# One projection of a hybrid encoder layer by seven products instead of eight, its operands' sums made by accumulating DMAs

## The chip, the core and the metric

The kernel runs on one core of a Trainium2 chip. The metric is the device time of one execution in microseconds (us), taken as the median of several runs. A profile of one further execution shows what each engine did: TensorE (PE, with its weight loads as PEld), VectorE (DVE), ScalarE (ACT), GpSimd (POOL) and SyncE (SP), which issues most DMAs.

## What is computed

One layer on x of 1024 positions by 1024 channels, in float32. Cut to what the change touches, the reference is:

```python
proj = jnp.einsum("bsd,de->bse", h, w_in)          # h = rmsnorm(x)
a = ...                                            # convolution branch, to 1024 channels
o = _bi_hgrn2(q, v, z_f, z_b, lb[0], lb[1])        # 8 heads of 128, both directions
of = o * lax.rsqrt(jnp.mean(o * o, axis=-1, keepdims=True) + EPS)
bmix = of * norm_w * jax.nn.silu(og)
bmix = jnp.einsum("bse,ed->bsd", bmix, o_w)        # the o projection
y = jax.nn.sigmoid(g_a) * a + jax.nn.sigmoid(g_b) * bmix
x = x + jnp.einsum("bsd,de->bse", y, w_out)
...                                                # feed-forward block, final norm
```

## The kernel before

All activations are kept transposed: a tile has 128 channels on the partitions and 512 positions (one half of the sequence) along it. A product with a weight column of 128 channels is a sum over 8 tiles of channels. Float32 accuracy is had by splitting each operand into a high and a low part (`split`, L124: a cast on ScalarE, a subtraction on VectorE), and by three matmuls for each pair (`mm3`, L144: lines 149 to 151). The input projection and the feed-forward block already use seven products for a block of two by two (`pair_job`, L283), with sums of weights and of activations as operands; the o projection doesn't.

The program runs in stages. After the input projections come the scans: 8 heads, two halves each. Their matmuls are woven with pieces of the remaining input projections and of the convolution's last product (`dense`), and a head's outputs (`outputs`, `scan_outputs`) follow one head later. There, GpSimd places four blocks of a half's scores by four small DMAs (L1371, tile `S`), makes the norm factors (L575 and L576, tile `ors`), ScalarE scales by them (L1452), PE turns the tiles (L1460), and VectorE applies gain and gate (L1462). The result is written to `d_bm[h][half]` by SP, the last head's is split at once; `bm_loads` brings the other heads back and splits them.

The o projection follows (L1590 and on): a job for each of the 8 output tiles, for each half 8 rows of three matmuls into a bank `mm` of PSUM. `merge` (L1571) loads the gate `d_gb` and the gated convolution branch `d_a`, multiplies and adds on VectorE and splits the result into `mg`, which the w_out stage reads. Beside these jobs `weight_sums` makes the sums of weights for the first three jobs of the feed-forward block, by VectorE, and stores them in `d_us`.

The order on PE is the order of the program (L91). On the other engines a scheduler sets it when the kernel is built, and each engine then works through its list in order, its DMA issues included. `later(n, do)` (L159) puts work n pieces of the matmul stream ahead in the program; `run_jobs` (L195) prepares the next job's weights while one runs. Pools with a fixed number of buffers (`wr` and `wp` for weights, `hx`, `ev`, `tm` and others for tiles) let a new tile wait for the last reader of an old one.

Of the kernel before, what the change touches and what calls it, by code (L numbers as in the profile page):

```python
# [21 lines left out]
CONV_FILL = 1.53  # L22
NPAIRS = 19
LN_MEAN = 5
GLU_FIRST = 4
GLU_LEAD = 6
GLU_FILL = 2
# [21 lines left out]
def tile_hybrid_encoder(  # L49
# [74 lines left out]
    def split(hi, lo, src, eng, late=False):  # L124
        parts = A.copy(hi, src), eng.tensor_tensor(lo, src, hi.bitcast(F32), op=ALU.subtract)  # L125
# [438 lines left out]

    def in_cols(c0):
        return w_cols(w_in, 0, ND, c0)


    NK2 = ND // 2
# [625 lines left out]

    last_keys, last_turned, last_scaled = [], [], []

    kscale = cp.tile([P, 2 * NH], F32, name="kscale")
    V.tensor_scalar(kscale, lbw[:, 3, :], DK**-0.5, None, op0=ALU.mult)

# [214 lines left out]
    def scan_outputs(h, kept, Sf, Sb):  # L1415


        ons, gates = [None, None], [None, None]
        ss = cp.tile([P, 2, 4], F32, name=nm("oss"), tag="oss", bufs=2)
        rs = cp.tile([P, 2, 4], F32, name=nm("ors"), tag="ors", bufs=2)  # L1420
        for half in (1, 0):
            S_t, v, qF = kept[half]
            o = bank("ob")
            for c in range(4):
                sl = slice(c * P, (c + 1) * P)
                g = half * 4 + c
                terms = [(S_t[:, c, :], v[:, c, :])]
                if g > 0:
                    terms.append((qF[:, 1, sl], Sf[half][:, c, :]))
                if g < 7:  # L1430
                    terms.append((qF[:, 0, sl], Sb[half][:, c, :]))
                for n, (l, r) in enumerate(terms):
                    T.matmul(o[:, sl], l, r, start=(n == 0), stop=(n == len(terms) - 1))  # L1433
            on = tmp()
            A.copy(on, o)
            for c in range(4):
                junk = hp.tile([P, DK], F32, tag="jk", name=nm("jk"), bufs=1)
                A.activation(  # L1438
                    junk, on[:, c * P : (c + 1) * P], AF.Square, accum_out=ss[:, half, c : c + 1]
                )  # L1440
            ons[half] = on
            gates[half] = page(hp, "og", 2)
            nc.sync.dma_start(gates[half], d_og[h][half])
            if half == 1:
                yield
        rstd_small(rs, ss, DK)
        yield
        yield
        for half in range(2):
            for c in range(4):  # L1450
                sl = slice(c * P, (c + 1) * P)
                done = A.activation(  # L1452
                    ons[half][:, sl], ons[half][:, sl], AF.Copy, scale=rs[:, half, c : c + 1]
                )
            last_scaled[:] = [done]
            yield
        for half in range(2):
            b = bank("tr")
            for c in range(4):
                T.transpose(b[:, c * P : (c + 1) * P], ons[half][:, c * P : (c + 1) * P], ident)  # L1460
            bt = ev()
            V.scalar_tensor_tensor(bt, b, vec("hn", h), gates[half], op0=ALU.mult, op1=ALU.mult)  # L1462
            if h == NH - 1:
                bm[h][half] = split(hx(), hx(), bt, V)
            else:
                nc.sync.dma_start(d_bm[h][half], bt)
            yield

    class Base:
# [29 lines left out]
        yield  # L1499
        yield from scan_outputs(h, kept, Sf, Sb)  # L1500

    bm = [[None, None] for _ in range(NH)]

    def bm_loads(half):
        for h in range(NH - 1):
            t = page(hp, "A", 8)
            nc.sync.dma_start(t, d_bm[h][half])
            behind = last_turned if h < NH - 2 else last_scaled
            with tc.issue_after(behind[0].ins):
                bm[h][half] = split(hx(), hx(), t, V)  # L1510

    NI = 2 * NH
    cur = Base(scan_inputs(0))
# [42 lines left out]
    for steps, pieces in TAIL:  # L1556
        pending.fill(steps)
        dense.fill(pieces)
    bm_loads(0)
    pending.fill(1)  # L1560
    dense.drain()
    bm_loads(1)
    pending.drain()
    hp.release()

# [5 lines left out]
    def merge(i):  # L1571
        def evac(half, acc):
            sb, a = ev(), tmp()
            for t, src in ((sb, d_gb), (a, d_a)):
                nc.sync.dma_start(t, src[i][half])
            V.tensor_tensor(sb, acc, sb, op=ALU.mult)
            V.tensor_tensor(a, a, sb, op=ALU.add)
            mg[i][half] = split(
                page(p4, "mg", 4 * ND, F32R), page(p4, "mg", 4 * ND, F32R), a, V
            )  # L1580

        return evac

    def o_cols(i):
        return w_cols(hgrn_o_w, 0, NH, i * P)

    def bm_of(k, half):
        return bm[k][half]

    o_jobs = [duo_job(o_cols(0), o_cols(1), NH, bm_of, merge(0), merge(1))]  # L1590
    o_jobs += [std_job(o_cols(i), NH, bm_of, merge(i)) for i in range(2, ND)]

    def column_halves(w, r0, nk, c0, c1):
        return [w_cols(w, r0, 2 * nk, c) for c in (c0, c1)]

    def up_cols(j):
        return column_halves(ffn_w_up, 0, ND // 2, j * P, DFF + j * P)
# [4 lines left out]
    def weight_sums(r, o, nk, d):  # L1602
        cols = nk * P

        def piece(src=None):
            t = page(fw, "h7", 2 * NK2)[:, :cols]
            if src is not None:
                nc.sync.dma_start(t.rearrange("p (k e) -> p k e", e=P), src)
            return t

        r0, o0, o1, r1 = piece(r[:, :nk]), piece(o[:, :nk]), piece(o[:, nk:]), piece(r[:, nk:])

        def sums():
            c0 = piece()
            todo = ((c0, r0, o0), (o1, o0, o1), (r0, r0, o1), (r1, r1, r0))
            for q, (t, a, b) in enumerate(todo):
                V.tensor_tensor(t, a, b, op=ALU.add)
                nc.sync.dma_start(d[:, q], t)

        return sums  # L1620

    s_o = Stream(run_jobs(o_jobs))
    todo = [(*up_cols(n), ND // 2, d) for n, d in enumerate(d_us)]
    for n, args in enumerate(todo):
        s_o.fill(16 if n else 8)
        later(5, weight_sums(*args))
    s_o.drain()
    advance_chores(1 << 10)

# [497 lines left out]
```

## Time and profile before

| | |
|---|---|
| median of 3 runs | 1707.12 us (1706.96 to 1707.62) |
| the profiled execution | 1706.98 us |
| its span | 1705.0 us |
| PE busy | 1688.6 us, 11719 instructions |
| DVE, ACT, POOL busy | 1269.3, 827.3, 245.9 us |
| mean granted PE clock | 0.999 |
| moved by DMA | 306.17 MB, 180 GB/s |

A row of a timeline has the start in us, the duration, the engine, the line, the operation, the tiles written and read with a count, and in brackets the engine's idle time before it with what ended it. A line of the DMA table has what is written from what, the issuing engine, the number of issues, the size of one, and the median us from issue to landing. Line numbers are those of the kernel before unless the text says otherwise.

### The profile page before, as it was taken

To read this page: it belongs to the slowest core of one execution; us is meant where nothing else is said; L and a number is where in the kernel's file an instruction comes from. 1 tells how busy PE (TensorE), PEld (TensorE's weight loads), DVE (VectorE), ACT (ScalarE), POOL (GpSimd) and SP (SyncE) were. 2 spreads that over 40 slices of the span, in tenths; PEclk is the share of its full clock that TensorE was granted. 3 is DMA by queue.
4 is the path that set the end of the run, shared out by engine and by line. 5 is a ranking of instruction groups with operands and counts; after the bars stand their busy time and mean duration, and the time that the engine had idled before them with its cause. 6 is when DMAs were issued, how large, how long until landed. Compare 5 with 4: busy or idle time off the path is not lost.

```text
span 1705.0 us, 30406 instructions
## 1 busy us (share of the span) xinstructions
PE 1688.6 (99%) x11719; PEld 1408.2 (83%) x11719; DVE 1269.3 (74%) x1938; ACT 827.3 (49%) x1562; POOL 245.9 (14%) x287
## 2 busy tenths in 40 slices
PE   9999999999999999999999999999999999999998
PEld 6788888888888888888888888888888888888787
DVE  5889899887678888888565467676777776657865
ACT  7454343335476777776432345444344434442334
POOL 1312222200001111111100003122222222000110
PEclk9999999999999999999999999999999999999999
DMA  7887887866573444436797455686777776773842
GB/s 240 284 213 186 191 196 172 205 187 206 165 236 100 139 129 134 129 116 221 241 294 243 128 167 176 153 171 143 172 164 178 164 183 149 237 260 102 212 98 99
DMA packets 332871, 306.17 MB, mean 180 GB/s; under 512 B 17454, under 2 KB 244918, under 8 KB 332726
## 3 DMA queue, kind: packets, MB, share of 16 engines
q1 hardware_dynamic: 285366, 265.42, 48.8%
q0 software_dynamic: 47360, 38.81, 15.4%
q8 instruction: 92, 1.51, 0.4%
q14 instruction: 53, 0.43, 0.1%
HBM read 201.40 MB, written 84.93 MB: 168 GB/s over the span
## 4 chain that ended last, share of the span: by engine, by line
PE 70%; ACT 1%; DVE 1%; DMA 0%; issue 0%; POOL 0%; POOLq 0%; ACTq 0%; DVEq 0%
PE mm L149 16%; PE mm L151 16%; PE mm L150 16%; PE sc L149 3%; PE sc L150 3%; PE sc L151 3%; PE ob L1433 2%; PE tr L149 2%; PE tr L150 2%; PE tr L151 2%; PE sc L1247 1%; PE sc L1333 1%; PE mm L1392 1%; PE sc L1392 1%; PE ob L1247 1%; PE tr L1382 0%
## 5 line engine op out<-in xcount | busy, mean ns | idle before, releaser
L149 PE MATMUL mm<-hx,wp 128*128 128x512 f32 x1068 | 425.7, 399 | 0.0
L151 PE MATMUL mm<-hx,wp 128*128 128x512 f32 x1068 | 417.0, 390 | 0.5 <-DVE wp L125 0.5
L150 PE MATMUL mm<-hx,wp 128*128 128x512 f32 x1068 | 416.2, 390 | 0.6 <-POOL hx L125 0.6
L125 ACT CAST wp<-wr 128x1024 fp32r<-128x1024 f32 (+2 forms) x146 | 146.9, 1006 | 224.3 <-PE mm L150 165.0
L151 PEld LDWEIGHTS mm<-hx,wp 128*128 128x128 f32 x1068 | 200.5, 188 | 44.6 <-DVE wp L125 1.6
L149 PEld LDWEIGHTS mm<-hx,wp 128*128 128x128 f32 x1068 | 200.6, 188 | 40.6 <-ACT wp L125 0.2
L150 PEld LDWEIGHTS mm<-hx,wp 128*128 128x128 f32 x1068 | 200.8, 188 | 39.9 <-POOL hx L125 1.0
L125 DVE TENSOR_TENSOR wp<-wr,wp 128x1024 fp32r<-128x1024 f32 (+2 forms) x144 | 169.5, 1177 | 39.8 <-ACT wp L125 39.4
L1065 DVE SCALAR_TENSOR_TENSOR acc<-gl,v_b,acc 128x1024 f32<-128x1024 f32 x120 | 153.5, 1280 | 1.7
L441 ACT COPY su<-mm 128x512 f32<-128x512 f32 x82 | 47.8, 583 | 84.4 <-PE mm L151 84.3
L1371 POOL DMA_DIRECT2D S<-D x64 | 36.1, 571 | 281.1 <-ACT jk L1438 125.3
L125 ACT CAST wq<-sw 128x1024 fp32r<-128x1024 f32 x41 | 43.2, 1054 | 61.3 <-PE mm L150 32.9
L1194 DVE TENSOR_TENSOR qF<-qF,tb 128x512 f32<-128x512 f32 x96 | 65.9, 686 | 9.5 <-ACT A L1228 8.9
L149 PE MATMUL tr<-hx,wp 128*128 128x512 f32 x180 | 70.1, 390 | 0.0
L151 PE MATMUL tr<-hx,wp 128*128 128x512 f32 x180 | 70.1, 389 | 0.0
L150 PE MATMUL tr<-hx,wp 128*128 128x512 f32 x180 | 70.0, 389 | 0.0
L1194 DVE TENSOR_TENSOR kG<-kG,tb 128x512 f32<-128x512 f32 x96 | 65.9, 687 | 4.0 <-ACT A L1228 2.2
L1710 DVE SCALAR_TENSOR_TENSOR tm<-gp,v_a,tm 128x512 f32<-128x512 f32 x88 | 66.0, 750 | 3.3 <-ACT tm L1708 1.3
L302 POOL DMA_DIRECT2D sw<-in_ffn_w_up_dram x38 | 49.8, 1502 | 116.0 <-DMA sw<-in_ffn_w_up_dram 72.4
L149 PE MATMUL sc<-hy,wq 128*128 128x512 f32 x164 | 63.9, 390 | 0.0
L151 PE MATMUL mm<-hy,wp 128*128 128x512 f32 x164 | 63.8, 389 | 0.0
L149 PE MATMUL mm<-hy,wp 128*128 128x512 f32 x164 | 63.8, 389 | 0.0
(377 smaller groups left out, 3721.9 us busy)
## 6 DMA issues: line engine op xcount, KB each, us to landing
wr<-in_w_in_dram SPq DMA_DIRECT2D x48, 512.0 KB, 5.6
wr<-in_ffn_w_up_dram SPq DMA_DIRECT2D x22, 512.0 KB, 5.6
sw<-in_w_in_dram SPq DMA_DIRECT2D x38, 256.0 KB, 3.1
d_g<-ft SPq DMA_DIRECT2D x38, 256.0 KB, 2.0
sw<-in_ffn_w_up_dram SPq DMA_DIRECT2D x38, 256.0 KB, 3.2
sw<-in_ffn_w_up_dram POOLq DMA_DIRECT2D x38, 256.0 KB, 6.7
wr<-sw POOLq DMA_DIRECT2D x32, 256.0 KB, 3.2
wr<-wr POOLq DMA_DIRECT2D x32, 256.0 KB, 3.3
```

What stands on the lines that cost most here:

```text
L125: parts = A.copy(hi, src), eng.tensor_tensor(lo, src, hi.bitcast(F32), op=ALU.subtract)
L149: T.matmul(acc, whi[:, k, :], ahi, start=first, stop=False, skip_group_check=again)
L150: T.matmul(acc, whi[:, k, :], alo, start=False, stop=False, skip_group_check=again)
L151: T.matmul(acc, wlo[:, k, :], ahi, start=False, stop=last, skip_group_check=again)
L302: G.dma_start(o, a, accum_op=ALU.add)
L441: A.copy(t, acc)
L1065: V.scalar_tensor_tensor(acc, g[:, k : k + S], tap(k), acc, op0=ALU.mult, op1=ALU.add)
L1194: return V.tensor_tensor(o, a, b, op=op)
L1247: T.matmul(b[g, o], A_t[:, at : at + 32], Q_t(at), start=True, stop=True)
L1371: G.dma_start(S_t[g : g + 32, :, g : g + 32], D_t[g : g + 32])
L1392: T.matmul(u[:, sl], kTs[d][:, sl], v[:, c, :], start=True, stop=True)
L1710: V.scalar_tensor_tensor(c, g[:, o + k : o + k + H], vec("fdw", k * NF + j), c, op0=ALU.mult, op1=ALU.add,)
```

## The change

The o projection is written as seven products. With the operand's tiles in blocks (heads 0 to 3 and 4 to 7 by the two halves) and the weights in blocks (input rows by output columns), each product takes 4 rows for one of four pairs of output tiles (tile p and tile p + 4). They are run product by product over the four pairs: 1, 2 and 6 for all pairs, then 7 and 4 pair by pair, then 5 and 3. A group of two items shares one weight page.

- In the scan stage, `sums_by_dma` makes the sums of weights, for the four pairs (`d_os`) and the three feed-forward jobs (`d_us`), seven sums in all: a piece is loaded, other pieces are added to it by accumulating DMAs that GpSimd issues, and each sum is stored by SP. `weight_sums` is gone.
- The gains get signs (`less`), all heads' results go to `d_bm`, and `bm_loads` brings back one half only.
- The sums of activations are made in `chain` from `d_bm` by accumulating DMAs too (`plus`), each followed by a split (`operand`): product 7, then 6, then 4 from the same page, and 5 from another; 3 is a block as it is.
- Product 7 is copied by ScalarE, and product 4 accumulates in its bank. `merge` adds `d_a` by an accumulating DMA.

```diff
+    d_os = [dp.tile([P, 4, ND // 2 * P], F32, name=f"d_os_{n}") for n in range(ND // 2)]
...
-            V.scalar_tensor_tensor(bt, b, vec("hn", h), gates[half], op0=ALU.mult, op1=ALU.mult)
-            if h == NH - 1:
-                bm[h][half] = split(hx(), hx(), bt, V)
-            else:
-                nc.sync.dma_start(d_bm[h][half], bt)
+            gain = vec("hn", h) if (h < NK2) == (half == 1) else less[:, h : h + 1]
+            V.scalar_tensor_tensor(bt, b, gain, gates[half], op0=ALU.mult, op1=ALU.mult)
+            nc.sync.dma_start(d_bm[h][half], bt)
...
+    def sums_by_dma(at, r, o, d):
...
+        def piece(src):
+            t = hp.tile([P, NK2, P], F32, tag="ws", name=nm("ws"), bufs=2)
+            nc.sync.dma_start(t, src)
+            return t
...
+        def more(t, src):
+            G.dma_start(t, src, accum_op=ALU.add)
+        def keep(n, t):
+            nc.sync.dma_start(q(n), t)
+        todo = (
+            lambda: ts.extend((piece(a11), piece(a21))),
+            lambda: (more(ts[0], a21), more(ts[1], a22)),
+            lambda: (keep(0, ts[0]), keep(1, ts[1])),
+            lambda: more(ts[1], a11),
+            lambda: keep(2, ts[1]),
+            lambda: more(ts[1], a12),
+            lambda: keep(3, ts[1]),
+        )
+        for n, do in enumerate(todo):
+            later(at + SUMS_GAP * n, do)
...
+    def merge(e, p, half, x0, x1=None, op=None):
+        i = p + e * NK2
+        t = next(gates_of)()
+        nc.sync.dma_start(t, d_gb[i][half])
...
+            V.tensor_tensor(both, x0, x1, op=op)
+            V.tensor_tensor(t, both, t, op=ALU.mult)
+        G.dma_start(t, d_a[i][half], accum_op=ALU.add)
+        mg[i][half] = split(mg_page(), mg_page(), t, V)
...
+    def plus(t, src):
+        G.dma_start(t, src, accum_op=ALU.add)
...
+    for k in range(NK2):
+        chain.append(raw_page(d_bm[k][1]))
+        plus(chain[k], d_bm[k + NK2][1])
+        if k == 0:
+            operand(2, NK2 - 1, raw_page(d_bm[NH - 1][0]))
+        operand(7, k, chain[k])
+        plus(chain[k], d_bm[k][0])
+        operand(6, k, chain[k])
+    def fourth(k):
+        plus(chain[k], d_bm[k + NK2][0])
+        operand(4, k, chain[k])
+    def fifth(k):
+        t = raw_page(d_bm[k][1])
+        plus(t, d_bm[k][0])
+        operand(5, k, t)
+    def third(k):
+        operand(3, k, raw_page(d_bm[k + NK2][1]))
+    for n, do in enumerate((fourth, fifth, third)):
+        for k in range(NK2):
+            later(10 + 8 * n + 2 * k, lambda do=do, k=k: do(k))
+    o_items = [(i, p) for i in (1, 2, 6) for p in range(NK2)]
+    o_items += [(i, p) for p in range(NK2) for i in (7, 4)]
+    o_items += [(i, p) for i in (5, 3) for p in range(NK2)]
...
+                if i == 7:
+                    seventh[p] = page(fw, "h7", 2 * NK2)
+                    A.copy(seventh[p], acc)
```

The scheduler places the new DMAs as follows. GpSimd's list in the scan stage, from the first half's `S` to the fifth's, before (lines of the kernel before; `x4` is four such rows):

```order
L1371 DMA S_763_4801<-D_715_4539 32x4x32 x4
L1371 DMA S_807_5107<-D_748_4767 32x4x32 x4
L1371 DMA S_856_5424<-D_797_5078 32x4x32 x4
L575 TENSOR_SCALAR ors_874_5547<-oss_873_5546 128x8
L576 TENSOR_TENSOR ors_874_5547<-ors_874_5547,mhalf_73 128x8
L1371 DMA S_916_5798<-D_841_5390 32x4x32 x4
L1371 DMA S_969_6135<-D_906_5769 32x4x32 x4
```

The same list now, from the third half's `S` to the fifth's (lines of the changed kernel; `ws_1342` and `ws_1343` are the sixth sum's tiles, `ws_1489` and `ws_1490` the seventh's):

```order
L1385 DMA S_860_5451<-D_801_5100 32x4x32 x4
L1538 DMA ws_1343_8466<-in_ffn_w_up_dram 128x4x128
L1538 DMA ws_1489_9381<-in_ffn_w_up_dram 128x4x128
L586 TENSOR_SCALAR ors_878_5575<-oss_877_5574 128x8
L587 TENSOR_TENSOR ors_878_5575<-ors_878_5575,mhalf_73 128x8
L1538 DMA ws_1343_8466<-in_ffn_w_up_dram 128x4x128
L1538 DMA ws_1490_9383<-in_ffn_w_up_dram 128x4x128
L1538 DMA ws_1343_8466<-in_ffn_w_up_dram 128x4x128
L1538 DMA ws_1490_9383<-in_ffn_w_up_dram 128x4x128
L1385 DMA S_920_5828<-D_845_5417 32x4x32 x4
L1538 DMA ws_1490_9383<-in_ffn_w_up_dram 128x4x128
L1385 DMA S_975_6173<-D_910_5799 32x4x32 x4
```

All 28 adds of the weights stand ahead of the fifth half's `S`, wherever the program has them, and most of a sum's adds ahead of the first head's `ors`. Each add waits for a load or a store of the same tile. The two buffers of `ws` are used so that the first sum has a tile in each, and of the others every other sum has the same one, its two tiles one after the other.

At the start of the o projection GpSimd's list had nothing before. Now it stands there, from product 7's last row on (`xq_1736`, `xq_1744`, `xq_1749` and `xq_1754` are the chain's pages of rows 0 to 3; adding `d_bm_k_0` for k below 4 makes product 6's operand, adding `d_bm_4_0` and so on product 4's; `xq_1803` and `xq_1804` are for product 5; `d_a` is a merge's):

```order
L1646 DMA xq_1754_10714<-d_bm_7_1_283 128x512
L1646 DMA xq_1736_10672<-d_bm_0_0_268 128x512
L1646 DMA xq_1736_10672<-d_bm_4_0_276 128x512
L1634 DMA ev_1778_10828<-d_a_0_0_140 128x512
L1646 DMA xq_1744_10690<-d_bm_1_0_270 128x512
L1646 DMA xq_1803_10946<-d_bm_0_0_268 128x512
L1634 DMA ev_1783_10855<-d_a_1_0_142 128x512
L1646 DMA xq_1744_10690<-d_bm_5_0_278 128x512
L1646 DMA xq_1804_10963<-d_bm_1_0_270 128x512
L1646 DMA xq_1749_10702<-d_bm_2_0_272 128x512
```

Row 2 of product 6 stands behind product 4's add to row 1, which waits for the split of product 6's row 1; row 3 likewise stands further down, behind product 4's add to row 2.

ScalarE's list at the first product 7, now (`hx_1830` and `hx_1834` are product 3's last operands, `h7_1817` the copy):

```order
L126 CAST wp_1810_11009<-wr_1802_10931 128x1024
L126 CAST hx_1830_11088<-xq_1829_11086 128x512
L126 CAST hx_1834_11108<-xq_1833_11106 128x512
L1732 COPY h7_1817_11035<-ob_1813_11016 128x512
L126 CAST wp_1825_11066<-wr_1807_10972 128x1024
```

The copy of product 7 stands behind those casts, which wait for their loads.

More of the change, by code (lines that the diff above doesn't have):

```diff
@@ L24 @@
 LN_MEAN = 5
+SUMS_GAP = 3
 GLU_FIRST = 4
@@ L1196, in tile_hybrid_encoder @@
     last_keys, last_turned, last_scaled = [], [], []
+    less = cp.tile([P, NH], F32, name="less")
+    o_hn = vec_off["hn"][1]
+    V.tensor_scalar(less, vecs["v_a"][:, o_hn : o_hn + NH], -1.0, None, op0=ALU.mult)
     kscale = cp.tile([P, 2 * NH], F32, name="kscale")
@@ L1569, in tile_hybrid_encoder @@
     mg = [[None, None] for _ in range(ND)]
[L1571 to L1585, printed above, removed]
@@ L1599, in sums_of @@
+    s_o = Stream(run_jobs([o_job(g) for g in range(len(o_groups))]))
     def sums_of(d, nk):
         return [d[:, q : q + 2].rearrange("p q (k e) -> p (q k) e", e=P) for q in (0, 2)]
[L1602 to L1626, printed above, removed]
     s_o.drain()
```

105 lines of the change are left out of this document (91 added, 14 removed).

## The prediction

> **What bounds the kernel now.** I read the page first, then TensorE's waits, then the stretches around the o projection.
>
> ```profile
> span 1705.0 us, 30406 instructions
> PE 1688.6 (99%) x11719; PEld 1408.2 (83%) x11719; DVE 1269.3 (74%) x1938; ACT 827.3 (49%) x1562; POOL 245.9 (14%) x287
> DMA  7887887866573444436797455686777776773842
> PE 70%; ACT 1%; DVE 1%; DMA 0%; issue 0%; POOL 0%; POOLq 0%; ACTq 0%; DVEq 0%
> ```
>
> TensorE (PE) is busy for 99% of the span and carries the chain. Its waits, longest first, begin so:
>
> ```profile
> PE mm L502 <- DMA vr<-in_attn_norm_w_dram: 2.3, 1, 2.3
> PE tr L1382 <- DVE kG L1194: 1.4, 2, 1.1
> ```
>
> So there is no slack that could pay back a wait: a matmul less is time won, and every us in which PE waits for a new operand is lost, wherever it falls.
>
> **The matmuls removed.** The w_out stage has the old o projection's shape, 384 matmuls of 128x512:
>
> ```profile
> L149 PE MATMUL mm<-mg,wp x128: 389/389/389, 954.9 to 1041.3; 128*128 128x512 f32 x128
> L125 ACT CAST mg<-tm x16: 620/622/625, 877.3 to 956.6; 128x512 fp32r<-128x512 f32 x16
> L125 DVE TENSOR_TENSOR mg<-tm,mg x16: 682/692/694, 877.9 to 957.6; 128x512 fp32r<-128x512 f32 x16
> 867.38 0.60 PE L1460 MATMUL tr<-ident,tm 128*128 128x128 f32 x4
> 867.73 0.49 PE L149 MATMUL mm<-hx,wp 128*128 128x512 f32 x1
> ```
>
> One of every three matmuls stands in the first row: (1041.3 - 954.9) / 127 / 3 = 0.2268 us each. The o projection begins at 867.73 behind the last transposes, w_out's first matmul starts at 954.9, so it lasts 87.2 us. Seven products of 4 rows for 4 pairs make 7 x 4 x 4 x 3 = 336 matmuls: 48 fewer, -10.9 us. One product (12 matmuls) lasts 2.72 us.
>
> **Product 4 straight behind product 7.** It accumulates in the bank that ScalarE's copy of product 7 must first read. Such a copy today:
>
> ```profile
> 1112.59 0.39 PE L151 MATMUL sc<-h,wq 128*128 128x512 f32 x1
> 1112.82 0.39 PE L149 MATMUL mm<-hx,wq 128*128 128x512 f32 x1
> 1113.07 0.59 ACT L441 COPY su<-sc 128x512 f32<-128x512 f32 x1 [2.03 <-PE sc L151]
> ```
>
> The last matmul of a product starts at 1112.59, the copy ends at 1113.66; the next matmul, which could start at 1112.82, would wait until about 1113.7. That is 0.9 us, four times: +3.6 us. Today another product lies between, so nobody waits.
>
> **The accumulating DMAs, prices.** All the new sums go through POOL's queue, and the order prints waits on them, so the durations to landing decide:
>
> ```profile
> A<-d_bm SPq DMA_DIRECT2D x14, 256.0 KB, 4.5
> ev<-d_gb SPq DMA_DIRECT2D x16, 256.0 KB, 2.6
> xr<-d_x POOLq DMA_DIRECT2D x16, 256.0 KB, 4.4
> sw<-in_ffn_w_up_dram SPq DMA_DIRECT2D x38, 256.0 KB, 3.2
> sw<-in_ffn_w_up_dram POOLq DMA_DIRECT2D x38, 256.0 KB, 6.7
> sw<-in_ffn_w_up_dram POOLq DMA_DIRECT2D x1, 256.0 KB, 4.8
> wr<-sw POOLq DMA_DIRECT2D x32, 256.0 KB, 3.2
> d_ga<-ev SPq DMA_DIRECT2D x12, 256.0 KB, 2.4
> S<-D POOLq DMA_DIRECT2D x64, 16.0 KB, 2.7
> 1217.07 1.30 POOL L302 DMA_DIRECT2D sw<-in_ffn_w_up_dram  x1 [5.24 <-DVE gp L1741]
> 1226.52 0.89 POOL L302 DMA_DIRECT2D wr<-sw  x1 [6.20 <-DVE wp L125]
> 1230.05 0.86 POOL L302 DMA_DIRECT2D wr<-wr  x1 [2.64 <-DMA wr<-sw]
> ```
>
> The last two rows show the rule of the queue: the second add starts 3.53 us after the first, when that has landed, and until then POOL does nothing else. An add of a 128x4x128 weight piece is the `sw` row of POOLq: 6.7 us in the median, 4.8 for the first of a pair. An add of a contiguous page from HBM is the `xr` row, 4.4.
>
> The Trainium skill, "DMA: Bandwidth & Descriptors", section "Anatomy of one DMA — SWDGE (gpsimd) path", fits 2.0 us plus the bytes by 436e3 per us, which for 256 KB would be an estimated 2.6 us. The trace does not agree: every 256 KB add from HBM here takes 4.4 or more; by that figure the two terms below would shrink as the first rival says.
>
> **The o projection's operands.** The sums for products 7, 6, 4 and 5 are made by such adds, in POOL's order shown with the change. The first load of `d_bm` stands on SP behind the last stores of the stage before, which wait for these:
>
> ```profile
> 868.15 1.37 DVE L1156 TENSOR_TENSOR ev<-mm,ev 128x512 f32<-128x512 f32 x2
> 870.04 0.74 DVE L1462 SCALAR_TENSOR_TENSOR ev<-tr,v_a,og 128x512 f32<-128x512 f32 x1
> ```
>
> In the new order the last L1167 (today's L1156) follows the second of these: 870.8 + 0.7, so the store goes at about 871.6 and the loads from 872.0. With 3.5 us for a load (between 2.6 and 4.5) the first add is issued at 875.6. A split costs 0.62 + 0.69 and some hand-over, 1.4. Then, by 4.4 per add and 0.87 per issue: row 0 of product 7 lands at 880.0, is split by 881.4; row 0 of product 6 issued 881.5, lands 885.9, split by 887.3; only now does POOL get past product 4's add (887.4) and the gate's, to row 1 of product 6 at 889.1, which is split by 894.9; product 4's second add waits for that (895.0), row 2 of product 6 follows at 896.7, split by 902.5; product 4's third add 902.6, row 3 of product 6 at 903.5, split by 909.3. PE wants that last operand at 867.7 + 8 x 2.72 + 3 x 0.68 = 891.5. It stands 17.8 us: +17.8 us. Four landings and splits in a row make it; at 3.2 per add (`wr<-sw`) 13, at 6.7 27.
>
> Next, ScalarE's copy of the first product 7 stands, by the printed order, behind the casts of product 3's operands, whose loads need pages that product 5's sums free last. It may be late by nothing or by the load, the cast and the queue ahead of them (up to 5 us): +4.5 us, nearer to that end as those sums follow row 3 of product 6. At the end w_out wants the last merged tile 5.44 + 2.04 = 7.5 us after the last product, and the gate's multiplication, its add (4.4) and the split need about 7: 0 to 4 us, taken as +2. The vector adds removed from this stretch lie beside PE: 0. Together -10.9 + 3.6 + 17.8 + 4.5 + 2 = +17.0 us.
>
> **The weights' sums in the scan stage.** POOL today, the first two heads:
>
> ```profile
> 536.41 2.29 POOL L1371 DMA_DIRECT2D S<-D  x4 [16.28 <-ACT S L1369]
> 557.47 2.18 POOL L1371 DMA_DIRECT2D S<-D  x4 [18.77 <-ACT jk L1438]
> 565.09 0.25 POOL L575 TENSOR_SCALAR ors<-oss 128x8 f32<-128x8 f32 x1 [5.44 <-ACT jk L1438]
> 565.42 1.66 POOL L576 TENSOR_TENSOR ors<-ors,mhalf 128x8 f32<-128x8 f32 x1
> 567.12 0.40 ACT L1452 ACTIVATE tm<-tm,ors 128x128 f32<-128x128 f32 x1 [1.42 <-POOL ors L576]
> 574.14 0.63 ACT L1228 COPY A<-kG 128x512 f32<-128x512 f32 x1
> 574.79 0.60 PE L1460 MATMUL tr<-ident,tm 128*128 128x128 f32 x4
> 480.81 0.48 SPq L1214 DMA_DIRECT2D zi<-d_z  x1
> ```
>
> Now the first accumulate of the seventh sum stands ahead of the first `ors`. The sums share two buffers, every other one in the same, so one buffer has half a sum (the first one's second tile), then the third and fifth sums, then that add. A sum is 2 loads, 4 adds and 4 stores, one after another: 2 x 3.2 + 4 x 4.8 + 4 x 2.4 and ten hand-overs of 0.1 = 36.2 us. I take 4.8, the nearest row for an add that is mostly alone, since the page's DMA tenths are 3 to 4 from 511 us on (7 in the slice before) and 6 to 8 where the 6.7 was measured. The loads follow the `zi` load, at 481.7: 3.3 + 1.3 + 3 x 7.3 = 26.5 gives 508.2, two sums 580.6, a load 584.0, the add's issue 585.3, `ors` ready 587.3 against 567.1: 20.2 late. ScalarE waits there in order and, behind the `ors` scaling, has the copies (574.14) that PE needs next, with some 2 us in hand: +18 us. A second wait, for the `S` of the next half, falls inside the same delay. Ends: with 3.2 per add +1, with 6.7 +39. SP's loads are held up by the same stores, but were issued two halves ahead: 0.
>
> **Sum.** The profiled execution took 1706.98 us for its span of 1705.0 (median 1707.12): 1707.0 + 17.0 + 18 = **1742 us**.
>
> **The rivals.** *The adds land faster.* At `wr<-sw`'s 3.2 the scan stage loses 1 us; the four landings in the o projection are 4.8 shorter and the copy's extra wait goes, so that stage costs +8: 1716 us. For it speaks that half of the new traffic falls into quiet stretches; against it that no add from HBM lands so fast here. By the Trainium skill's 2.6 us (the page named above) it would be a few us less still.
>
> *POOL is not held up (faster).* If the adds with their waits were handed over to the DMA queues at once, product 6's operands would come before 891.5, from which point only the removed matmuls and the copies count: 1707.0 - 10.9 + 3.6 = 1699.7 us. Against it speak the 2.64 us before the 1230.05 row.
>
> *The adds crowd each other.* Two buffers' chains and SP's loads overlap; at 6.7 per weight add the scan stage costs 39: 1707.0 + 39 + 17 = 1763 us. For it: the median row; against: the quiet tenths.
>
> **How the numbers follow.** The forecast gets 0.60 (its own range 1726 to 1758), the faster landings 0.17, the crowd 0.15, the free queue 0.08. 1712 to 1768 leaves out the free queue and about half the crowd's upper side. 0.2% (3.4 us) is about what a measurement of this kernel tells from no change; faster by more 0.09, within 0.02, slower 0.89.
>
> **What would show it.** In the new profile PE should wait (1) in the scans for ScalarE's `ors` scaling, `ors` itself ready some 20 us later against the scan than today and POOL waiting for DMAs on `ws`; (2) in product 6's first pair for `hx` splits, one wait per row, 18 us in all; (3) 0.9 us at each product 4; and the o projection should last some 102 us where it lasts 87.2 today. No such waits on POOL, or weight adds landing in 3 us, would make me wrong; a total below 1712 would mean that both are hidden.

## The result, and the profile after

The changed kernel takes 1799.81 us (median of 4 runs, 1795.9 to 1804.83) against 1707.32 us: a ratio of 1.0543, with a 95% interval of 1.0517 to 1.057. The forecast was 1742 us, from 1712 to 1768: the direction was right, the size much too small. The profiled execution took 1804.83 us for a span of 1802.9, which is 97.9 longer than before's 1705.0; it is the longest of the four executions.

The page of the changed kernel, in the rows shown of before, with the granted TensorE clock:

```profile
span 1802.9 us, 30537 instructions
PE 1700.8 (94%) x11671; PEld 1410.7 (78%) x11671; DVE 1273.5 (71%) x1941; ACT 846.0 (47%) x1592; POOL 310.8 (17%) x347
PEclk9999999999997799999996999999999999999999
```

There are 48 matmuls fewer (x11671 for x11719), but PE's share fell from 99% to 94%, and in two places the granted clock fell too. TensorE's waits, longest first, show which:

```profile
PE mm L150 <- ACT hx L126: 25.4, 3, 11.8
PE ob L1447 <- DMA S<-D: 20.3, 1, 20.3
PE tr L1592 <- DMA tm<-d_v: 16.2, 1, 16.2
PE sc L1261 <- ACT A L1242: 6.6, 4, 3.7
PE ob L150 <- ACT h L1732: 5.7, 2, 3.3
```

Before, the longest was 2.3 us. The stages' ends, from PE's timeline (the last transposes of the scans, the first matmul of w_out):

```profile
922.93 0.60 PE L1474 MATMUL tr<-ident,tm 128*128 128x128 f32 x4
923.28 0.48 PE L150 MATMUL mm<-hx,wp 128*128 128x512 f32 x1
1044.99 0.39 PE L150 MATMUL mm<-mg,wp 128*128 128x512 f32 x1
```

With the rows of before (867.73 and 954.9), the loss of 97.9 us is: the scan stage 923.28 - 867.73 = 55.6; the o projection 121.7 for 87.2, so 34.5; all that follows 7.8. Predicted were 18, 15 and 2.

**The scan stage.** GpSimd, with the `D` of the second half that its `S` needs (VectorE), the `ors` row and ScalarE's wait for it:

```profile
540.78 0.29 DVE L1325 COPY_PREDICATED D<-m,sc 128x128 f32<-128x128 uint8 x1
567.23 2.79 POOL L1385 DMA_DIRECT2D S<-D  x4
613.09 0.20 POOL L586 TENSOR_SCALAR ors<-oss 128x8 f32<-128x8 f32 x1
615.07 0.41 ACT L1466 ACTIVATE tm<-tm,ors 128x128 f32<-128x128 f32 x1 [24.68 <-POOL ors L587]
574.13 0.77 PE L1447 MATMUL ob<-v,S 128*128 128x128 f32 x2 [20.30 <-DMA S<-D]
```

The second half's `D` is whole at 541.1, but its `S` is issued at 567.23 (536.41 before), because GpSimd stands at adds of the weights' sums; PE, which takes this half first, waits 20.3 us. `ors` comes at 613.09 instead of 565.09, 48.0 us late; PE was 24.9 us behind by then (its last stop begins at 596.44, and the row that ends it started at 571.57 before), so that is some 23 us against the scan. ScalarE's copies for PE stand behind the scaling by `ors`: they are the 6.6 us of waits at L1261. SP is held as well. Its waits, two of its rows, and the load of `v` before with its first reader:

```profile
SPq L1541 <- DMA ws<-in_hgrn_o_w_dram: 58.7, 16, 7.5
SPq L1541 <- DMA ws<-in_ffn_w_up_dram: 40.9, 11, 7.2
604.29 0.32 SPq L1541 DMA_DIRECT2D d_us<-ws  x1
608.64 0.94 SPq L119 DMA_DIRECT2D tm<-d_v  x2
612.67 1.12 PE L1592 MATMUL tr<-ident,tm 128*128 128x128 f32 x4 [16.23 <-DMA tm<-d_v]
```

```profile
559.87 0.93 SPq L118 DMA_DIRECT2D tm<-d_v  x2
571.57 0.60 PE L1544 MATMUL tr<-ident,tm 128*128 128x128 f32 x4
```

A store of a sum waits in SP's list until the add before it has landed, 99.6 us in all, and the loads of `v` stand behind. Before, that load was issued only 11.7 us ahead of its reader.

**The adds.** The DMA table, adds (POOLq) and stores:

```profile
ws<-in_hgrn_o_w_dram POOLq DMA_DIRECT2D x16, 256.0 KB, 5.8
d_os<-ws SPq DMA_DIRECT2D x16, 256.0 KB, 2.3
xq<-d_bm POOLq DMA_DIRECT2D x16, 256.0 KB, 6.6
ws<-in_ffn_w_up_dram POOLq DMA_DIRECT2D x12, 256.0 KB, 5.1
```

The weights' adds take 5.1 and 5.8 us (4.8 assumed), those of `d_bm` 6.6 (4.4 assumed). The Trainium skill, "DMA: Bandwidth & Descriptors", section "Anatomy of one DMA — SWDGE (gpsimd) path", would have 2.6, an estimate by its fit. The trace does not agree.

**The o projection.** PE's stops at product 6's first pair, and at the four products 4:

```profile
958.66 0.79 PE L150 MATMUL mm<-hx,wp 128*128 128x512 f32 x1 [7.59 <-ACT hx L126]
972.44 0.79 PE L150 MATMUL mm<-hx,wp 128*128 128x512 f32 x1 [11.83 <-ACT hx L126]
980.33 0.79 PE L150 MATMUL mm<-hx,wp 128*128 128x512 f32 x1 [5.95 <-ACT hx L126]
...
983.78 0.60 PE L151 MATMUL mm<-hx,wp 128*128 128x512 f32 x1
984.21 0.41 PE L152 MATMUL mm<-hx,wp 128*128 128x512 f32 x1
984.46 0.40 PE L150 MATMUL mm<-hx,wp 128*128 128x512 f32 x1
...
997.44 0.50 PE L150 MATMUL ob<-mg,wp 128*128 128x512 f32 x1 [3.26 <-ACT h L1732]
1005.42 0.50 PE L150 MATMUL tr<-mg,wp 128*128 128x512 f32 x1 [0.68 <-ACT h L1732]
1011.84 0.50 PE L150 MATMUL tr<-mg,wp 128*128 128x512 f32 x1 [0.68 <-ACT h L1732]
1020.01 0.50 PE L150 MATMUL ob<-mg,wp 128*128 128x512 f32 x1 [2.42 <-ACT h L1732]
```

Rows 1 to 3 of product 6 come one landing after the other, as the order had it: 25.4 us. Their four adds were not alike. The first, issued by itself at 942.24, landed 4.6 us later; the other three, each issued within 0.6 us of another add, took 8.3, 8.7 and 5.6. The DMA engines weren't busier there: their mean share (packet times added up, so it can pass 1) was 1.09 during the 4.6 us and 0.89 and 0.86 during the 8.3 and 8.7. The rows from 980.33 show something more. Behind a stop, matmuls start 0.43 us apart instead of 0.2268, until 984.21. A table by stretches says why; its first three rows cover all the time at a lowered clock in this stage:

```profile
943.26:946.67 3.41, 3.19 (x8) 0.50 1.08 226
953.50:984.22 30.72, 7.78 (x15) 0.50 0.89 189
997.88:1001.29 3.41, 3.41 (x10) 0.50 0.02 6
985.00:986.00 1.00, 1.00 (x6) 1.00 1.03 188
```

(Stretch, length, PE's busy time and matmuls, granted clock, DMA share, GB/s.) The clock is 0.50 until 984.22 and then 1.00 again. In the 3.88 us from 980.33 8 matmuls started that take 1.81 us at the full clock: 2.1 us more for one stop. In the three stretches PE is busy for 14.4 us, so half the clock costs some 7.2 us. The sum of the stage closes only with it: 336 x 0.2268 = 76.2 of matmuls, 25.4 of waits for product 6, 7.0 for the copies of product 7 (the brackets of the last four rows), some 3 for split weights, and 121.7 - 111.6 = 10 us, of which 7.2 are the half clock and the rest small pieces, such as the end of a matmul at each stop. The Trainium skill, "TensorE: Matmul & The Clock Gate", section "Part 1: The HAM clock gate (the 'warmup' mystery)", states that the array runs at half rate after an idle window of about 3.4 us, until it has been busy for about as long. The trace agrees on the length: slow stretches last 3.41 us or about a multiple of it (30.72 is nine times as long). It does not agree that a whole idle window is needed, since stops of 2.35 us (ending at 942.22) and 3.26 us (at 997.44) had half the clock behind them too, and the one of 2.42 us at 1020.01 had not.

### The profile page after: what moved, and what is told of

Its sections match the earlier page's. It is cut to its first block, busy times and chain, and to the rows that moved or that the text cites. A ratio compares the mean times of both kernels' runs of the same rounds, so it can differ in the third digit from the quotient of the medians.

```text
span 1802.9 us, 30537 instructions
## 1 busy us (share of the span) xinstructions
PE 1700.8 (94%) x11671; PEld 1410.7 (78%) x11671; DVE 1273.5 (71%) x1941; ACT 846.0 (47%) x1592; POOL 310.8 (17%) x347
## 5 line engine op out<-in xcount | busy, mean ns | idle before, releaser
L150 PE MATMUL mm<-hx,wp 128*128 128x512 f32 x976 | 392.7, 402 | 25.4 <-ACT hx L126 25.4
L151 PE MATMUL mm<-hx,wp 128*128 128x512 f32 x976 | 383.2, 393 | 1.8 <-issue 1.2
L152 PE MATMUL mm<-hx,wp 128*128 128x512 f32 x976 | 383.1, 393 | 0.5 <-DVE wp L126 0.5
L126 ACT CAST wp<-wr 128x1024 fp32r<-128x1024 f32 (+2 forms) x150 | 151.1, 1007 | 231.8 <-PE mm L151 163.1
L150 PEld LDWEIGHTS mm<-hx,wp 128*128 128x128 f32 x976 | 184.5, 189 | 64.5 <-ACT hx L126 27.1
L152 PEld LDWEIGHTS mm<-hx,wp 128*128 128x128 f32 x976 | 184.5, 189 | 41.7 <-DVE wp L126 1.8
L151 PEld LDWEIGHTS mm<-hx,wp 128*128 128x128 f32 x976 | 184.7, 189 | 39.4 <-issue 1.6
L126 DVE TENSOR_TENSOR wp<-wr,wp 128x1024 fp32r<-128x1024 f32 (+2 forms) x148 | 174.4, 1178 | 56.7 <-ACT wp L126 53.2
L150 PE MATMUL tr<-hx,wp 128*128 128x512 f32 x200 | 78.5, 393 | 2.3 <-ACT wp L126 2.3
L152 PE MATMUL tr<-hx,wp 128*128 128x512 f32 x200 | 78.7, 394 | 0.5 <-DVE wp L126 0.5
L151 PE MATMUL tr<-hx,wp 128*128 128x512 f32 x200 | 78.3, 392 | 0.0
```

The costliest lines, as they stand in the source:

```text
L150: T.matmul(acc, whi[:, k, :], ahi, start=first, stop=False, skip_group_check=again)
L151: T.matmul(acc, whi[:, k, :], alo, start=False, stop=False, skip_group_check=again)
L152: T.matmul(acc, wlo[:, k, :], ahi, start=False, stop=last, skip_group_check=again)
```

## Experiments

The theory after the result: nothing in the change is slow by itself; three in-order lists (GpSimd's, SP's and, in the o projection, those of GpSimd and ScalarE) hold other work behind accumulating DMAs, and most stops of PE of over 2 us cost their length and 1 to 3 us more by half clock. Rivals: the traffic of the sums; SP alone; GpSimd alone. The table has each run's loss by stage against before (start of the o projection against 867.73; its length against 87.21; the rest of the span, 1705.0 - 954.94, against 750.06), from one profiled execution each. The times are those of one execution, except for the changed kernel, e10, e11 and e13 (medians of 4). Single executions of the changed kernel differ by up to 9 us, and a stage that an edit leaves alone varies too: the scans lie between +50.4 and +58.2 in the changed kernel, e3, e4 and e7, the o projection between +32.1 and +35.9 in the changed kernel, e1, e2, e5, e6, e8 and e9.

| kernel | us | scans | o projection | rest |
|---|---|---|---|---|
| changed kernel | 1799.81 | +55.6 | +34.5 | +7.8 |
| e1 sums wholly on GpSimd | 1821.87 | +70.8 | +34.9 | +9.4 |
| e2 weights' sums by VectorE | 1766.34 | +17.9 | +32.3 | +9.4 |
| e3 activations' sums by VectorE | 1786.91 | +58.2 | +13.9 | +7.9 |
| e4 7, 7, 4, 4 | 1795.92 | +50.4 | +30.0 | +8.6 |
| e5 S and ors elsewhere | 1812.96 | +61.6 | +35.9 | +8.6 |
| e6 as e5, sums on GpSimd | 1751.20 | +4.3 | +32.1 | +8.1 |
| e7 six ahead of four | 1803.98 | +54.2 | +34.5 | +8.3 |
| e8 only SP held | 1808.89 | +56.8 | +33.7 | +11.6 |
| e9 sums between the ors | 1757.57 | +7.0 | +33.6 | +10.1 |
| e10 e9, e3 and e4 | 1735.91 | +6.6 | +12.6 | +10.3 |
| e11 e10, gates by VectorE | 1722.66 | +4.5 | +5.9 | +4.1 |
| e12 e10 without addends | 1731.08 | +7.7 | +10.8 | +5.8 |
| e13 e11, fours behind six | 1716.31 | +6.0 | +1.8 | +2.8 |

**e1: who holds the scans.**

```diff
-            nc.sync.dma_start(t, src)
+            G.dma_start(t, src)
...
-            nc.sync.dma_start(q(n), t)
+            G.dma_start(q(n), t)
```

> The changed kernel with one edit: the loads and stores of the weights' sums are issued by GpSimd too, no longer by SP. In the changed kernel the scan stage is 55.6 us longer than before. Theory SP (its stores of sums wait for an add to land, 99.6 us in all, and the loads of zi and v that the scans need stand behind them): those loads come on time, the waits for zi and for tm<-d_v go, and the scan stage is at most 20 us longer than before, total near 1765. Theory GpSimd (S and ors stand behind adds that wait, as the prediction had it): GpSimd now waits for six more transfers per sum, so S and ors come later than in the changed kernel and the stage is still 55 us longer or more, total 1800 or above, with PE's waits on S<-D and on ors.

The scan stage became 70.8 us longer. PE's waits:

```profile
PE ob L1447 <- DMA S<-D: 36.3, 1, 36.3
PE tr L1474 <- ACT tm L1466: 20.5, 1, 20.5
```

With SP free the wait for `v` is gone, but `S` and then the scaling by `ors` are later than ever. So GpSimd's list, lengthened by the sums' other transfers, is enough for the whole loss, and SP isn't needed for it.

**e8: SP alone.** The other half of that question. First tried as e5, with the small DMAs of `S` on ScalarE's queue and `ors` on VectorE without its power:

```diff
-            G.dma_start(S_t[g : g + 32, :, g : g + 32], D_t[g : g + 32])
+            nc.scalar.dma_start(S_t[g : g + 32, :, g : g + 32], D_t[g : g + 32])
...
-        rstd_small(rs, ss, DK)
+        V.tensor_scalar(rs, ss, 1.0 / DK, EPS, op0=ALU.mult, op1=ALU.add)
```

> The changed kernel with the small DMAs of S issued by ScalarE and the norm factors ors made by VectorE without their power of -1/2 (so the outputs of the scans are scaled wrongly): nothing that PE waits for stands in GpSimd's list in the scan stage any more; SP still issues the sums' loads and stores and is held by them. The scan stage was 55.6 us longer than before: some 22 us at S of the second half, 17 at the load of v and at ors. If GpSimd's list is what delays it, the wait on S goes and the stage is 15 to 35 us longer than before, by the load of v on SP alone. If SP's waits are behind both stalls, it is still 45 us longer or more.

It decided nothing, as the edit brought a wait of its own. ScalarE's waits:

```profile
ACT kT L1399 <- DMA q<-d_q: 20.2, 1, 20.2
ACT A L1242 <- DMA d_us<-ws: 19.9, 1, 19.9
```

ScalarE stood at its issues of `S`, and what ended these waits were landings of SP's DMAs that have nothing to do with `S`. So SP's delay passed over to ScalarE. In e8 VectorE copies `S`'s blocks, and no DMA changes its queue:

```diff
-            G.dma_start(S_t[g : g + 32, :, g : g + 32], D_t[g : g + 32])
+            V.tensor_copy(S_t[g : g + 32, :, g : g + 32], D_t[g : g + 32])
```

> The changed kernel with S's blocks copied by VectorE instead of by small DMAs, and the norm factors made by VectorE without their power of -1/2 (the scans' outputs are scaled wrongly): GpSimd's list holds up nobody in the scan stage, no DMA is moved to another queue, and SP is still held by the sums' stores. If SP's waits alone cost time, the loads of zi and v come late and the scan stage is 15 to 45 us longer than before, with PE waiting behind those loads. If they are hidden by issuing the loads two halves ahead, as the prediction had it, it is at most 8 us longer.

```profile
PE tr L1592 <- DMA tm<-d_v: 31.8, 1, 31.8
PE sc L1406 <- ACT kT L1399: 9.9, 1, 9.9
PE ob L1447 <- DVE D L1376: 9.1, 1, 9.1
```

The two shorter waits come from SP as well: ahead of them ScalarE stood 12.3 us for a load of `zi` (until 556.00) and 13.4 us for a store of `d_ga` (until 637.60). 56.8 us, more than the range's upper end: SP's stores alone delay the loads as much as both lists together did in the changed kernel. The two delays lie side by side there, and freeing GpSimd alone brings nothing. (Freeing SP alone could not be had without lengthening GpSimd's list, as e1 did.)

**e6 and e2: is it the traffic?** e6 is e5 and e1 together: the same bytes, but whoever waits for sums holds up nobody.

> As the kernel with S and ors elsewhere (again without the power), and the sums' loads and stores issued by GpSimd as well: the same 28 adds, 14 loads and 28 stores move the same bytes, but neither SP nor GpSimd holds up anything that the scans need. If only the queues that wait make the loss, the scan stage is at most 8 us longer than before. If the traffic itself slows other transfers down, it is 25 us longer or more.

The scan stage is 4.3 us longer than before: the queues made the loss, not the traffic. Nor was the traffic spread thin: from 480 to 680 us the DMA engines' mean share was 0.86 to 0.94 in stretches of 50 us, where the changed kernel had 0.65 to 0.93 and the kernel before 0.39 to 0.55. e2 keeps SP's loads and stores but lets VectorE add, with addends in halves (there is room for one small buffer):

```diff
         def more(t, src):
-            G.dma_start(t, src, accum_op=ALU.add)
+            for c in (0, 2):
+                x = hp.tile([P, NK2 // 2, P], F32, tag="wx", name=nm("wx"), bufs=1)
+                nc.sync.dma_start(x, src[:, c : c + 2])
+                V.tensor_tensor(t[:, c : c + 2], t[:, c : c + 2], x, op=ALU.add)
...
-            lambda: (more(ts[0], a21), more(ts[1], a22)),
+            lambda: (V.tensor_tensor(ts[0], ts[0], ts[1], op=ALU.add), more(ts[1], a22)),
```

One addend of each sum is in a tile already, so 21 addends are loaded, in 42 halves, and not the 28 of the text that follows.

> The changed kernel with the weights' sums added by VectorE: no accumulating DMA in the scan stage, but the same sums, with addends loaded in halves through one small buffer. If the loss of 55.6 us comes from queues that wait for adds to land (SP's or GpSimd's), the stage is at most 8 us longer than before and the total near 1750. If it comes from the traffic of the sums itself (7 x 2 loads, 28 addends, 28 stores of 256 KB on busy DMA engines), the stage stays over 30 us longer, total above 1775.

+17.9 us, between the two expectations. VectorE now waits 18.7 us in its own list for the addends (11.6 and 7.1 us), and PE 9.1 for its `kG`; a short wait in the busiest list still costs.

**e9: the same sums, other places.** A complete kernel: sums wholly on GpSimd as in e1, `S` copied as in e8, and a sum of weights only behind each head's `ors`:

```diff
+        made = rstd_small(rs, ss, DK)
+        if h < len(sums_left):
+            sums_by_dma(1, *sums_left[h], behind=made)
...
+            with tc.issue_after(behind.ins):
+                do()
```

> A complete kernel: the same sums by the same accumulating DMAs, but their loads and stores on GpSimd, S's blocks copied by VectorE, and the order set by hand: two sums ahead of the first ors, then one behind each ors, so that GpSimd has some 43 us for the 30 to 40 us of a sum before the next ors. If only the place in the queues costs, the scan stage is at most 8 us longer than before, with the o projection as in the changed kernel: 1707 + 8 + 34 + 5 = 1746 to 1756. If ors comes late behind a sum that lasts over 43 us, PE waits at the scaling by ors and the total stays above 1770.

GpSimd's rows around a sum, its adds left out here:

```profile
612.49 1.66 POOL L587 TENSOR_TENSOR ors<-ors,mhalf 128x8 f32<-128x8 f32 x1
614.12 1.61 POOL L1533 DMA_DIRECT2D ws<-in_hgrn_o_w_dram  x2
...
652.53 0.56 POOL L1543 DMA_DIRECT2D d_os<-ws  x1 [6.99 <-DMA ws<-in_hgrn_o_w_dram]
655.25 0.20 POOL L586 TENSOR_SCALAR ors<-oss 128x8 f32<-128x8 f32 x1 [2.15 <-ACT jk L1452]
```

A sum lasts 39 us, ends 2.2 us ahead of the next `ors`, and the stage is 7.0 us longer than before; with no accumulating DMA exchanged for anything, 48.6 us of the 55.6 are gone. The total is 1.6 us above the expected range, by the rest of the program.

**e4 and e7: the o projection's order.**

```diff
-    o_items += [(i, p) for p in range(NK2) for i in (7, 4)]
+    o_items += [(i, p) for q in (0, 2) for i in (7, 4) for p in (q, q + 1)]
```

> The changed kernel with one table changed: products 7 and 4 run as 7, 7, 4, 4 for two pairs at a time, so that another product lies between a product 7 and the product 4 in its bank. The four waits for the copy are 3.4, 0.8, 0.8 and 2.6 us, 7.7 in all. If the copy itself is what they wait for, all four go: 7.7 us less in the o projection. If the copy stands behind casts of product 3's operands whose loads are late, only about 0.9 each goes and the two long ones keep 2.5 and 1.7: 3.6 us less. Total 1792 to 1797.

All waits for a copy of product 7 are gone, also the two long ones, but new ones came further on (1.7 us for a tile `h` that VectorE makes, 3.2 for split weights): 4.5 us less in the stage for 7.7 us of waits, which is 2.1 below the lowest of the kernels without this edit. In e10, with the same order, 3.4 us of waits for the copies are back. e7 holds product 4's and 5's adds, and the merges', behind product 6's (in that text and in e3's, stops are counted from start to start: 8.1 there is 7.59 in the brackets above):

```diff
+        with tc.issue_after(sixes[-1].ins):
+            do()
...
-        plus(chain[k], d_bm[k + NK2][0])
+        behind_six(lambda: plus(chain[k], d_bm[k + NK2][0]))
```

> The changed kernel with one thing changed: in the o projection the adds for products 4 and 5 and those of the gated branch are held behind product 6's last add in GpSimd's list, so that rows 1 to 3 of product 6 no longer wait for product 4's adds to the row before. The stage lasts 121.7 us in the changed kernel, with waits of 8.1, 12.5 and 6.6 us in product 6's first pair. Theory order (four landings in a row): one wait of some 8 us stays, since the first add of product 6 can't be issued before product 7's split, the other two go, with the slow matmuls behind them: 96 to 104 us. Rival, DMA engines (0.9 to 1.0 busy there): the adds land later as they are issued closer together, and the stage still lasts 112 us or more. The scan stage is as in the changed kernel.

The stage lasted 121.7 us again. GpSimd's first and second add for product 6, and two of PE's stops:

```profile
940.27 0.86 POOL L1646 DMA_DIRECT2D xq<-d_bm  x1 [3.94 <-DMA xq<-d_bm]
949.26 0.86 POOL L1646 DMA_DIRECT2D xq<-d_bm  x1 [8.13 <-DVE hx L126]
...
960.96 0.80 PE L150 MATMUL mm<-hx,wp 128*128 128x512 f32 x1 [4.98 <-ACT hx L126]
993.34 0.80 PE L150 MATMUL ob<-mg,wp 128*128 128x512 f32 x1 [11.23 <-ACT h L1738]
```

Product 6's stops halved (13.0 for 25.4 us), but they did not go: the second add waits for the split of product 7's second row, and ScalarE casts that row only behind product 6's first. The chain stood in two lists, and I had changed one. What was won came back at 993.34, where the copy of product 7 waits behind casts of pages that the held adds now bring later. Neither of the two expectations was right: the length is the rival's, but product 6's adds, now issued one at a time, landed in 6.1, 4.1, 4.1 and 4.3 us, mostly earlier than the 4.6, 8.3, 8.7 and 5.6 of the changed kernel, and not later.

**e3: VectorE adds.**

```diff
     def plus(t, src):
-        G.dma_start(t, src, accum_op=ALU.add)
+        x = page(fw, "h7", 2 * NK2)
+        nc.sync.dma_start(x, src)
+        V.tensor_tensor(t, t, x, op=ALU.add)
```

> The changed kernel with the sums of activations in the o projection added by VectorE to pages that SP loads; the scan stage and the merge's adds stay. The o projection lasts 121.7 us in the changed kernel. Theory landings (four landings and splits of product 6 in a row through GpSimd's list): the three waits of 8.1, 12.5 and 6.6 us and the slow matmuls behind them go, and it lasts 76.2 us of matmuls, 7.7 us of waits for the copies of product 7 and some 3 for the first weights: 87 to 90, total near 1765. Rival, loads: the pages come late from SP, whose first load of them waits for the last stores; then 16 more loads on SP leave half of the wait, and it lasts 100 us or more, total 1778 or above.

101.1 us: 20.6 less, but past the rival's border, by waits that neither expectation named. Product 6's operands are no longer waited for; the longest stops are now for split weights (3.4, 5.2, 2.4 us).

**e10 to e13: together, and what is left.** e10 is e9, e3 and e4.

> The sums between the ors, the sums of activations on VectorE, and 7, 7, 4, 4, together. If the three losses are separate, they add: the scan stage up to 8 us longer than before, the o projection 94 to 99 us (101 with the chain on VectorE, less some 4 for the copies of product 7), the end some 5 late: 1720 to 1733, still slower than before. If the late weights and operands in the o projection came only from queues delayed by the scan stage, it would last under 87 and the total would be under 1712.

It takes 1735.91 us (1.0168, 1.0151 to 1.0185): the scans and the o projection as expected or nearly (+6.6; 99.8 us), the rest 10.3 late, 3 us above the range. So e11 makes the merges' sums by VectorE too:

```diff
+        g = next(gates_of)()
+        nc.sync.dma_start(g, d_a[i][half])
...
-        G.dma_start(t, d_a[i][half], accum_op=ALU.add)
+        V.tensor_tensor(t, t, g, op=ALU.add)
```

> The kernel with all three, and the merges' gated branch loaded by SP and added by VectorE as before, so that no accumulating DMA is left in the o projection. With the adds the w_out stage and what follows lasted some 10 us longer than before, PE waiting 3.5 and 1.4 us for the last merged tiles and then running at a granted clock of 0.5 for a while. If the add's landing makes them late, 7 to 10 us go: 1726 to 1729. If the last tiles are late because the gates' loads are late (three more pages in use per pair of merges), nothing is gained or a few us lost: 1734 to 1740.

1722.66 us (1.0091, 1.0074 to 1.0107). The rest is 6.2 us shorter, nearly as the landing theory had it, and no wait for a merged tile is left; the o projection is 6.7 shorter, which neither expected. e12 is e10 with the addends' loads left out:

> The kernel with all three, but each sum of activations adds the page to itself: the 16 loads of 256 KB for the addends are left out (so the sums are wrong), the VectorE additions stay. The o projection lasted 99.8 us there, 23.6 above its matmuls, with the DMA engines 0.95 to 1.0 busy for its first 50 us. If the bytes bound that, the late weights come earlier and it lasts 84 to 92 us. If it is the order on SP and on ScalarE, it still lasts 96 us or more.

98.0 for 99.8 us: the bytes of these loads are not what binds. e13 takes e11 and holds products 4, 5 and 3 behind VectorE's last split for product 6:

```diff
+        with tc.issue_after(six_split[-1].ins):
+            do(k)
...
-            later(10 + 8 * n + 2 * k, lambda do=do, k=k: do(k))
+            later(20 + 6 * n + k, lambda do=do, k=k: held_by_six(do, k))
```

> The kernel with the gates on VectorE too, and one more order set by hand: the loads and additions for products 4, 5 and 3 are held behind VectorE's last split of product 6's weights, which stood behind seven of their instructions in its list. There the o projection lasted 93.1 us, with stops of 3.9, 3.1 and 6.4 us for split weights and slow matmuls behind them. If VectorE's order makes the stop of 6.4 and the one of 3.1 us, the stage lasts 80 to 86 us and the total is 1709 to 1716. If the loads of weights and pages bound it (DMA engines 0.8 to 1.0 busy), or product 4's operands then come late in their turn, it still lasts 90 us or more and the total is 1719 or above.

The stop of 6.4 us fell to 1.0, the stage to 89.0 us; the total is 1716.31 us (1.0049, 1.0033 to 1.0066), between the two expected ranges. PE's waits from the o projection on to 1000 us:

```profile
PE tr L150 <- ACT wp L126: 3.7, 1, 3.7
PE tr L152 <- DVE wp L126: 2.5, 1, 2.5
PE mm L152 <- DVE wp L126: 2.1, 1, 2.1
PE mm L152 <- DVE wp L1728: 1.0, 1, 1.0
```

That is 9.3 us of waits for split weights, 2.1 of them in w_out; in the o projection the clock was 0.50 from 893.00 to 899.83 and from 933.96 to 937.38 besides, with PE busy for 8.8 us of it, some 4.4 lost. Still no version beats the kernel before: 10.9 us of matmuls are saved, 6.0 are lost in the scans, 12.7 in the o projection and 2.8 behind it.

## Why the prediction was wrong

Most of the miss lies in the scan stage: it lost 55.6 us where 18 were forecast, and the whole profiled execution 97.9 where 35 were. The step that failed there is the one that put the second half's `S` at nothing.

- *The matmuls removed*, -10.9: right, 48 fewer at the same 0.2268 us.
- *Product 4 behind product 7*, 0.9 each and 4.5 more for the first copy, 8.1 in all: two stops were 0.7 us, the first and the last 3.3 and 2.4, 7.0 in all (7.7 from start to start). Right, except that the last copy was late too.
- *The o projection's operands*, +17.8: the mechanism was right, the size wrong. The working gave 27 at 6.7 us per add; the adds took 6.6 in the median, and the stops 25.4. The term that was mis-sized is the landing of product 6's four adds: 4 x 4.4 = 17.6 us in the working, 4.6 + 8.3 + 8.7 + 5.6 = 27.2 measured. 4.4 (`xr`) was about right for an add issued by itself (4.6 here, three of four at 4.1 to 4.3 in e7); three of the four stood right behind other adds, by the very order that the working went through, and for that it had no price. That 6.7 fits the stops so well is luck: it is the median of other adds. (Nor does every add from HBM take 4.4 or more in the kernel before, as the working says: that is a median, and single ones of `xr` took 3.9.)
- *The weights' sums*, +18 for 55.6. The stop that was priced came: `ors` was some 23 us late against the scan (20.2 in the working), and PE's stop of 16.2 us there (ended by the load of `v`) and the 6.6 us behind it make 22.8 where 18 were forecast. Two other steps failed. The adds ahead of the second half's `S` have no term. The working names one `S`, "the `S` of the next half", and lets its wait fall "inside the same delay"; for the `S` behind `ors` that held, as PE has no other wait for an `S` than the one of 20.3 us. But PE wants the second half's `S` from 553.8 on (574.13 - 20.30), some 43 us ahead of the stop that begins at 596.4 (612.67 - 16.23), so there were two stops and not one. And "SP's loads are held up by the same stores, but were issued two halves ahead: 0" was read from a load of `zi`; the load of `v` goes 11.7 us ahead, and e8 shows that SP alone costs 56.8. In the changed kernel this second delay is hidden beside GpSimd's (e1 has no wait for `v` and is no faster), so that step did not make the miss by itself; it would have made one with any cure for the other. Waits of 20.3, 16.2, 6.6 and 3.5 us (all waits of before were 2.6) and some 7.9 by the clock, with PE busy at 0.50 for 15.8 us, make up all but about 1 of the 55.6.
- *The end*, +2 for 7.8: the last merged tiles came late (3.4 us in two waits), and the half clock followed, from 1055.90 to 1062.73, with PE busy for 5.6 us of it, some 2.8 lost. e11, without these adds, has no such wait and gave 6.2 back; e12, which has them, varied by 4.5 as well, so the 6.2 are not exact.
- *What had no term*: the clock. PE worked at 0.50 for 35.8 us in all three stages behind its stops, which makes some 18 of the 97.9 us.
- *The rivals*: faster landings fell, and the free queue with them (in the scan stage GpSimd stood 33.9 us ahead of adds for stores of `d_os` to land). Crowded adds, at 1763, had the right direction and also missed the second half's `S`; the crowding showed in the o projection (8.3 and 8.7 us), where that rival had no price for it.

What stays open: why the e13 kernel's weights come late. Of the 12.7 us in its o projection the waits (7.2) and the clock (4.4) account for 11.6; of its 6.0 us in the scans 4.3 are short waits (6.9 for 2.6 before), which no run took apart. The order of the raw weights' loads on SP wasn't tried. Why an add behind another lands so late isn't shown either.

## What to carry to other kernels

An accumulating DMA costs its issuer little (0.86 us an issue in e7's rows) and its list much: ahead of pricing it, write down, for each list that waits for it (the issuer's, that of the store behind it, that of the cast behind it), the next instruction somebody needs and how many us in hand its reader has, tile by tile. When two lists are held at the same time, freeing one shows nothing; move the work to where every list has a gap as long as the whole sum (39 us here, between two `ors` that lie 43 apart). Price an add that is issued right behind another by one that was. And where PE is the path, a stop costs more than its length.

## What the runs showed of the hardware

- Behind stops PE was granted half its clock for some 3 to 7 us (3.9 behind the 5.95 us that end at 980.33; until 629.24 behind 3.68 us that end at 622.22 and 0.95 at 623.73). The kernel before, with no stop over 2.3 us, had 0.999.
- A DMA that ScalarE issues could wait there for DMAs that SP had issued for other tiles (20.2 us, ended by a load of `q`), in e5; in e6, where SP was never held, the whole scan stage was 4.3 us longer.
- The same 256 KB accumulating add from HBM took 5.1 to 6.6 us in the median. In the o projection it was 4.6 for one issued by itself, and 8.3 and 8.7 for two issued within 0.6 us of others.
- A 256 KB store took 2.6 to 4.9 us in the median in GpSimd's queue (e1, e6, e9) where SP's took 2.3 to 2.9.
